# Input stage of a hybrid attention and gating layer put in an order of its own; low weight parts moved from GpSimd to VectorE

## The chip, the cores and the metric

The kernel runs on one core of one Trainium2 chip. The time is the device time of one execution, in microseconds (us). TensorE is called PE in the rows, VectorE DVE, ScalarE ACT, GpSimd POOL, and the queue that issues every transfer SP.

## The reference

One layer over 2048 tokens of width 1024, in float32. One input projection feeds two branches, latent attention and a gated chunk-wise mixing; they are joined, projected and normed.

```python
proj = jnp.einsum('bsd,de->bse', h, w_in)
c_q, c_kv, k_rope, z_a, u, v, z_b = ...
q = rmsnorm(c_q) @ w_uq;  kv = rmsnorm(c_kv) @ w_ukv
q_rope, k_rope = rope(...), rope(...)
attn = causal_attention(concat(q_nope, q_rope), concat(k_nope, k_rope), val)
out_a = attn * silu(z_a)
v = layernorm(gelu(v))
sv = einsum('hts,bcshd->bcthd', tril(w_spatial), v in chunks of 128) + b_spatial
out_b = gelu(u) * sv * silu(z_b)
y = concat(out_a, out_b) @ w_out
return layernorm(alpha * x + y)
```

## The kernel before, in words

Nearly every operand of a product is split into a high part (a rounded copy, made by ScalarE) and a low part (the rest, made by a subtraction, `sub`, line 97), and each product is three matmuls: high by high, high by low, low by high. So each 512-column block of weights or activations that arrives costs one DMA, one ScalarE cast and one subtraction by VectorE or GpSimd.

**Input stage** (a block `ph1`; the first 560 us). It runs in two halves of 1024 tokens (`hf`), each with four parts. (1) The gating vector v: per chunk of 128 tokens 24 matmuls over 512 columns (`tok_mm`, line 791), a Gelu, mean and variance, `rsqrt` with three Newton steps of one-column instructions (`newton`, lines 110 to 112), two multiply-adds (814, 815), a split (821 and 97), 12 matmuls with the spatial weights (833) and four additions of the bias out of PSUM (836). (2) The feature tiles c = 0 to 7 (z_b, u), 24 matmuls over 512 columns each (`feat_mm`, line 798), an activation (942) and a gating product on GpSimd (950, 952). (3) The latents: per 128 tokens 24 matmuls over 416 columns (791 again), a copy (844), norm and rotation on VectorE (846 to 862), four transposes (868, 869) with splits of the result, and from these the queries of all heads (894, 913, 928), which are written to DRAM. (4) Eight more feature tiles (c = 8 to 11, z_a). At the end of the second half stands head 0's preparation: its keys (`k_unit`), the row maxima of its scores (`max_ops`, 352 with VectorE's 359 and 362) and twelve blocks of values (`v_unit`, 310).

These parts are written one after the other in program order (`v_step`, `c_step` with lags SLAG, VLAG, CLAG, and a list `fill` of which some entries are taken after each feature tile); the framework's scheduler then arranges the instructions on each engine. The subtractions for the weights run on GpSimd (`load_w`, `load_wide`), apart from four; those for x run mostly on VectorE. Weights and x pass through five buffers `raw`, so the next transfer waits for the subtraction that empties a buffer.

**Attention and the rest** (`ph2`) do not follow that scheduler: each step is an `Op` with an engine, a cost, a rank and what it depends on, and `issue` plays the program through: at each step it takes the operation that can start first, the lowest rank among near ties, and writes it. Its clock uses a table of costs (`LENGTH`, `LAG`), not the chip.

The lines quoted in the prediction by number are those of this kernel.

Of the kernel before, what the change touches and what calls it, by code (L numbers as in the profile page):

```python
# [56 lines left out]
def hybrid_layer_kernel(ctx: ExitStack, tc: tile.TileContext, xT, x, pos, w_feat, w_v, w_c,  # L57
# [14 lines left out]

    SLAG, VLAG, CLAG = 3, 5, 2
    SKEW, SPLIT, DEFER = 4, 4, 8

    UNITS, YSTART, VLATE = 36, 6, 12
    PREP = (3, 8)
    sb = ctx.enter_context(tc.tile_pool(name="sb", bufs=1))
# [29 lines left out]
    def newton(y, v, t):  # L108

        dve.tensor_scalar(out=t, in0=y, scalar1=y, scalar2=v, op0=ALU.mult, op1=ALU.mult)  # L110
        dve.tensor_scalar(out=t, in0=t, scalar1=-0.5, scalar2=1.5, op0=ALU.mult, op1=ALU.add)
        dve.tensor_scalar(out=y, in0=t, scalar1=y, scalar2=None, op0=ALU.mult)

    def rsqrt(y, v, t):
# [5 lines left out]
        for _ in range(3):  # L120
            for c in range(v.shape[-1]):
                newton(y[:, c:c + 1], v[:, c:c + 1], t[:, c:c + 1])
# [11 lines left out]
    def area16(shape, dt, name):  # L134
        return sb.tile(shape, dt, name=name, tag="area16")
# [30 lines left out]
    def load_kv_w():  # L166
        wkv = att["wkv"] = area12([P, 2, 2, 512], "wkv")
        for i, src in enumerate((w_uk, w_uv)):
            raw = raw2k([P, 512])
            sp.dma_start(out=raw, in_=src)  # L170
            act.copy(out=wkv[:, i, 0], in_=raw)
            sub(dve, wkv[:, i, 1], raw, f(wkv[:, i, 0]))

# [6 lines left out]
    def qs_(h):  # L180
        return q1 if h % 2 else att["q0"][0:DQK + 1]

    def q_alloc():
        att["q0"] = area16([P, 2, S], F32R, "q0")
# [5 lines left out]
    def kslot(h):  # L190
        return kt[h % 3]

    def k_init(i):
        for c in range(2):
            sp.dma_start(out=f(kt[i][NOPE:DQK, c, :]), in_=kr_d[c])
        pool.memset(f(kt[i][DQK:DQK + 1, 0, :]), 1.0)
# [4 lines left out]
    class Op:  # L201


        def __init__(self, eng, cost, rank, fn, deps, lag):
            self.eng, self.cost, self.rank, self.fn, self.lag = eng, cost, rank, fn, lag
            self.deps = [d for d in deps if d is not None]
            self.takes, self.end = [], None


    LENGTH = {"pe": (0.016, 1 / 2400), "act": (0.09, 0.00083), "dve": (0.065, 0.00104), "pool": (0.04, 0.00235),  # L210
              "sp": (0.35, 0.0)}
    LAG = {"pe": 0.2, "act": 0.13, "dve": 0.12, "pool": 0.12, "sp": 3.0}

    COUNT = {"a": 4, "c": 2, "pl": 5, "acc": 2, "acch": 1, "accl": 1, "bsb": 2, "opair": 4, "rb": 1, "raw": 5}

    def issue(ops):

        free = dict.fromkeys(LENGTH, 0.0)
        users, waits = {}, {}
# [5 lines left out]
        taken = {b: [] for b in COUNT}  # L225

        def put(o):
            ready[o.eng].append((max([d.end for d in o.deps], default=0.0), o))
# [4 lines left out]
        for _ in range(len(ops)):  # L233
            best = None
            for e, line in ready.items():
                can = []
                for at, o in line:
# [4 lines left out]
                    if at < float("inf"):  # L242
                        can.append((max(at, free[e]), o))
# [9 lines left out]
            free[o.eng] = t + o.cost  # L253
            o.end = t + o.cost + o.lag
# [6 lines left out]
    work = []  # L261

    def op(eng, n, rank, fn, deps=(), times=1):
        fixed, per = LENGTH[eng]
        o = Op(eng, times * (fixed + per * n), rank, fn, deps, LAG[eng])
        work.append(o)
        return o

    def now():

        for o in work:
            o.fn()
        work.clear()

    def k_ops(pr_, st, rank, deps=()):
# [4 lines left out]
        def mm():  # L280
            st_["x"] = bank_c()
            for i, (w, c) in enumerate(((0, 0), (1, 0), (0, 1))):
                pe.matmul(st_["x"], att["wkv"][:, 0, w, cs], ckv[:, c, ss], start=(i == 0), stop=(i == 2))
# [14 lines left out]
    def k_unit(pr_, st):  # L298
        k_ops(pr_, st, 0)
        now()  # L300

    def v_ops(g, b, rank, deps=()):
# [1063 lines left out]
```

## Time and profile before

| what | value |
|---|---|
| three runs | 1216.54, 1221.67, 1222.01 us, median 1221.67 |
| the profiled execution | 1217.24 us, of it span 1215.5 us |
| TensorE busy, mean granted clock | 1160.4 us, 0.978 |
| VectorE, GpSimd, ScalarE busy | 849.7, 609.4, 584.8 us |

A busy TensorE is not one at its best speed: at half the granted clock the same matmuls count as longer. What a stage can give is read from its idle time and its clock, and from what VectorE does meanwhile.

### The profile page before, as it was taken

To read this page: it belongs to the slowest core of one execution; us is meant where nothing else is said; L and a number is where in the kernel's file an instruction comes from. 1 tells how busy PE (TensorE), PEld (TensorE's weight loads), DVE (VectorE), ACT (ScalarE), POOL (GpSimd) and SP (SyncE) were. 2 spreads that over 40 slices of the span, in tenths; PEclk is the share of its full clock that TensorE was granted. 3 is DMA by queue.
4 is the path that set the end of the run, shared out by engine and by line. 5 is a ranking of instruction groups with operands and counts; after the bars stand their busy time and mean duration, and the time that the engine had idled before them with its cause. 6 is when DMAs were issued, how large, how long until landed. Compare 5 with 4: busy or idle time off the path is not lost.

```text
span 1215.5 us, 17544 instructions
## 1 busy us (share of the span) xinstructions
PE 1160.4 (95%) x5497; PEld 951.8 (78%) x5497; DVE 849.7 (70%) x2314; ACT 584.8 (48%) x1133; POOL 609.4 (50%) x564
## 2 busy tenths in 40 slices
PE   8899999999899999999999999999999879999997
PEld 6678898787688898867877887778777558878886
DVE  4965458525940196476989989889999993458966
ACT  4331412444211323425888878877888774422000
POOL 2353521245332602212979998888899866420000
PEclk9999999999999999997999999999999899999999
DMA  7320322554110503730021212211232224367541
GB/s 243 92 84 15 116 80 74 193 183 130 54 44 18 170 12 125 219 105 27 15 65 49 84 27 63 64 50 37 62 93 66 78 87 138 90 181 240 173 142 61
DMA packets 74765, 116.90 MB, mean 96 GB/s; under 512 B 17248, under 2 KB 21104, under 8 KB 74480
## 3 DMA queue, kind: packets, MB, share of 16 engines
q1 hardware_dynamic: 74672, 115.79, 30.7%
q8 instruction: 43, 0.70, 0.3%
q14 instruction: 50, 0.41, 0.1%
HBM read 79.38 MB, written 36.24 MB: 95 GB/s over the span
## 4 chain that ended last, share of the span: by engine, by line
PE 73%; DVE 14%; DMA 5%; ACT 3%; issue 2%; POOL 2%; SPq 1%; DVEq 0%; POOLq 0%; ACTq 0%
PE bank_a L798 19%; PE bank_a L1134 10%; PE bank_c L352 5%; PE bank_a L432 5%; PE bank_b L476 5%; PE bank_b L477 5%; PE bank_a L433 5%; PE bank_a L434 4%; PE bank_a L791 4%; PE bank_c L1134 4%; DMA raw<-in_xT_dram 2%; PE bank_a L913 2%; DVE gv L814 1%; PE bank_b L833 1%; PE bank_c L310 1%
## 5 line engine op out<-in xcount | busy, mean ns | idle before, releaser
L798 PE MATMUL bank_a<-xbuf,ring 128*128 128x512 f32 x1152 | 270.4, 390 | 0.0
L798 PEld LDWEIGHTS bank_a<-xbuf,ring 128*128 128x128 f32 x1152 | 214.3, 188 | 42.6
L463 POOL TENSOR_TENSOR acc<-acc,xbuf 128x512 f32<-128x512 f32 (+2 forms) x168 | 194.2, 1156 | 32.9 <-ACT xbuf L448 24.5
L442 ACT ACTIVATE bank_a<-bank_a 128x512 f32<-128x512 f32 (+1 forms) x288 | 162.9, 576 | 90.4 <-PE bank_a L434 45.9
L791 PE MATMUL bank_a<-ring,xbuf 128*128 128x512 f32 (+1 forms) x768 | 170.1, 381 | 12.1 <-ACT ring L686 5.7
L97 POOL TENSOR_TENSOR ring<-raw,ring 128x512 fp32r<-128x512 f32 (+1 forms) x76 | 100.4, 1339 | 148.5 <-ACT ring L680 108.7
L791 PEld LDWEIGHTS bank_a<-ring,xbuf 128*128 128x128 f32 x768 | 147.6, 194 | 30.5 <-ACT ring L686 5.7
L97 DVE TENSOR_TENSOR pl<-bank_a,xbuf 128x512 fp32r<-128x512 f32 (+1 forms) x192 | 125.6, 660 | 20.2 <-ACT xbuf L448 18.9
L362 DVE TENSOR_REDUCE mxt<-bank_c 128x1 f32<-128x512 f32 (+1 forms) x192 | 126.8, 666 | 11.6 <-PE bank_c L352 10.0
L477 PE MATMUL bank_b<-pl,xbuf 128*128 128x512 f32 (+1 forms) x320 | 119.6, 377 | 3.5 <-DVE pl L97 3.5
L448 ACT CAST xbuf<-bank_a 128x512 fp32r<-128x512 f32 (+1 forms) x192 | 107.1, 575 | 7.6 <-PE bank_b L476 0.4
L463 POOL TENSOR_TENSOR acc<-acc,ph 128x512 f32<-128x512 f32 (+1 forms) x72 | 85.0, 1181 | 11.7 <-ACT ph L448 8.0
L476 PE MATMUL bank_b<-xbuf 128*128 128x512 f32 (+2 forms) x216 | 82.1, 383 | 3.5 <-ACT xbuf L448 3.5
L942 ACT ACTIVATE act_t<-bank_a 128x512 f32<-128x512 f32 x48 | 28.5, 597 | 117.2 <-PE bank_a L798 117.0
L359 DVE CUSTOM_DVE_ANT_0 bank_c<-bank_c,maskq 128x256 f32<-128x256 f32 (+3 forms) x128 | 65.7, 518 | 13.1 <-PE bank_c L352 12.0
L477 PEld LDWEIGHTS bank_b<-pl,xbuf 128*128 128x128 f32 x320 | 62.2, 194 | 14.2 <-DVE pl L97 5.5
L97 DVE TENSOR_TENSOR pl<-bank_a,ph 128x512 fp32r<-128x512 f32 x96 | 65.1, 683 | 11.6 <-ACT ph L448 10.8
L97 DVE TENSOR_TENSOR xbuf<-raw,xbuf 128x512 fp32r<-128x512 f32 x42 | 33.8, 824 | 48.4 <-ACT xbuf L693 39.9
L432 PE MATMUL bank_a<-xbuf,ring 97*128 97x512 f32 (+2 forms) x160 | 62.0, 388 | 3.2 <-DVE pl L97 3.2
L352 PE MATMUL bank_c<-ring,q 96*128 96x512 f32 (+2 forms) x160 | 61.1, 405 | 3.1 <-DVE xbuf L97 1.6
L432 PE MATMUL bank_a<-q,ring 97*128 97x512 f32 (+2 forms) x160 | 63.0, 394 | 0.0
L352 PE MATMUL bank_c<-ring,xbuf 96*128 96x512 f32 (+2 forms) x160 | 60.1, 391 | 2.3 <-DVE mxt L362 0.9
(209 smaller groups left out, 2388.6 us busy)
## 6 DMA issues: line engine op xcount, KB each, us to landing
raw<-in_w_feat_dram SPq DMA_DIRECT2D x48, 256.0 KB
raw<-in_xT_dram SPq DMA_DIRECT2D x32, 256.0 KB
out_dram<-pl SPq DMA_DIRECT2D x32, 256.0 KB
raw<-in_w_v_dram SPq DMA_DIRECT2D x16, 256.0 KB
ob_d<-act_t SPq DMA_DIRECT2D x16, 256.0 KB
qn_d<-qh SPq DMA_DIRECT2D x16, 256.0 KB
qn_d<-ql SPq DMA_DIRECT2D x16, 256.0 KB
za_d<-act_t SPq DMA_DIRECT2D x16, 256.0 KB
```

What stands on the lines that cost most here:

```text
L97: eng.tensor_tensor(out=out_, in0=a, in1=b, op=ALU.subtract)
L352: pe.matmul(st_["x"][:, :hi - lo], qs_(h)[0:DQK, 0, qb * P:end], kslot(h)[0:DQK, 0, lo:hi], start=True, stop=True)
L362: dve.tensor_reduce(out=mx[h][:, qb, c:c + 1], in_=xps, axis=AX.X, op=ALU.max)
L432: pe.matmul(o_, k_[0:DQK + 1, 0, js], q_[0:DQK + 1, 0, qs], start=True, stop=False)
L442: act.activation(out=o_, in_=o_, func=AF.Exp, scale=SCALE)
L448: act.copy(out=un["ph"][:, c0:512], in_=un["x"][:, c0:512])
L463: pool.tensor_tensor(out=t_["acc"][:, cs], in0=t_["acc"][:, cs], in1=f(p_), op=ALU.add)
L476: pe.matmul(a_ps[:, cs], va, un["ph"][:, ps], start=first, stop=last)
L477: pe.matmul(b_ps[:, cs], vb, un["pl"][:, ps], start=first, stop=last and qt > 0)
L791: pe.matmul(dst[:, :n], a[:, k, js], b[:, 0:4, k, 0:cols], start=(k == 0 and i == 0), stop=(k == KT - 1 and i == 2))
L798: pe.matmul(dst, a[:, slot, k, :], b[:, k, :], start=(k == 0 and i == 0), stop=(k == KT - 1 and i == 2))
L1134: pe.matmul(y, mo(st, k, a)[:, js], wo(k, w)[:, ns], start=(k == kord(st)[0] and i == 0), stop=(k == kord(st)[-1] and i == 2))
```

## The change

All of the input stage is now made of `Op`s too (`manual_schedule`), with ranks from a running time T and costs from the same kind of table, and is played through once at its end (`issue(lead, SLACK)`): transfers may be taken up to 24 us before their rank and the others 16 us, and TensorE work counts as ready 1.2 us after another engine's result. The order of the parts: two feature tiles (c = 0 and 1 of the first 512 tokens) stand ahead of the gating vector; in the first half two z_a tiles stand among the latents; head 0's keys, queries, maxima and nine (not twelve) value blocks get ranks among the last eight z_a tiles, with small weight tiles of their own (`first_weights`); the other seven value blocks come early in attention. The low parts of all feature, v and latent weights and of all of x are made by VectorE; the spatial weights stay on GpSimd, and the full key and value weights go there. `newton` takes both columns of a statistic side by side. Two 16 KB areas become four of 8 KB, the ring of temporaries goes from 12 to 10 buffers with two more `held`, and a load of a head's queries becomes four DMAs where it was two. Attention keeps its rules, but with the new table (a DMA lag of 2.4 where it was 3.0) and with the clock of the input stage running on.

```diff
+    UNITS, YSTART, VLATE = 36, 6, 9
+    MIXLAG, SLACK = 8, 1.2
+    ZA = (3, 6), ()
+    PACE = 0.9
...
+    LENGTH = {"pe": (0.016, 1 / 2350), "act": (0.09, 0.00083), "dve": (0.065, 0.00104), "pool": (0.04, 0.00235),
+              "sp": (0.1, 0.0043)}
+    LAG = {"pe": 0.2, "act": 0.13, "dve": 0.12, "pool": 0.12, "sp": 2.4}
...
+    lead = {"sp": 24.0, "act": 16.0, "dve": 16.0, "pool": 16.0, "pe": 16.0}
...
+            at = [d.end + (slack if o.eng == "pe" != d.eng else 0.0) for d in o.deps]
+            ready[o.eng].append((max(at + [o.rank - lead[o.eng] if lead else 0.0]), o))
...
+            h_ = op("act", n, rank, lambda: act.copy(out=hi(), in_=st_["raw"]), [*last, *before, *deps])
+            l_ = op(eng, n, rank, lambda: sub(engines[eng], lo(), st_["raw"], f(hi())), [h_],
+                    times=1.1 if eng == "dve" else 1.05, pair=True)
+            d_.takes.append((home, [l_]))
...
-                sub(pool, wr_l[:, slot, ks, :], raw, f(wr_h[:, slot, ks, :]))
+                split_in(rank + 2 * q, [P, 4, P], w_feat[c][:, ks, :], lambda ks=ks: wr_h[:, slot, ks, :],
+                         lambda ks=ks: wr_l[:, slot, ks, :], "dve", [("w", slot, k) for k in range(4 * q, 4 * q + 4)])
...
+            g_ = op("act", 512, rank, gelu, [o])
+            s_ = op("dve", 512, rank, stats, [g_], times=4.2)
+            n_ = op("dve", 512, rank, norm, [s_, *of([("sg",)])], times=2.3, pair=True)
+            h_ = op("act", 512, rank, high, [n_], takes=[("tmp", mixed)] * 2)
+            l_ = op("dve", 512, rank, low, [h_], times=1.1, pair=True)
...
+                m_ = op("pe", 256, rank + MIXLAG, lambda half=half: mix(half), [h_, l_, *of([("wsp", half)])], times=7)
+                adds = [op("dve", 256, rank + MIXLAG, lambda half=half, e=e: add(half, e),
+                           [m_, *of([("bsp",), ("area8", t // 4)])]) for e in range(2)]
+                m_.takes.append(("b", adds))
...
+            k_ = op("act", 416, rank, keep, [o])
+            n_ = op("dve", 416, rank, norm, [k_, *of([("gc",), ("rope",)])], times=6.8)
+            t_ = op("pe", 128, rank, turn, [n_], times=6)
+            l_ = op("dve", 512, rank, lows, [h_], times=1.3)
...
+            order = ["f00", "f10", "v0", "v1", "v2", "v3", "v4", "v5", "v6", "v7", "f01", "f11"]
+            if hf == 1:
+                order = ["v0", "v1", "f00", "v2", "f10", "v3", "v4", "v5", "v6", "v7", "f01", "f11"]
...
+                k_ops(0, st, r, deps, "wk0")
...
+                        tops.append(max_ops(0, qb, c, r, [done["q"][0, st], *inits, *k_deps]))
+                        r += PACE * (hi - lo) / 512
...
+        first_head(T0)
+        issue(lead, SLACK)
```

The order on the engines at three places. First **VectorE at the end of the gating vector, first half**, before (`gate` is the mixed chunk with its bias, `vl` the low part of a normed chunk):

```order
L836 TENSOR_TENSOR gate<-bank_b,bsp_bc 64x2x128
L815 SCALAR_TENSOR_TENSOR gv<-gv,sm,sb_bc 128x512
L836 TENSOR_TENSOR gate<-bank_b,bsp_bc 64x2x128
L97 TENSOR_TENSOR vl<-gv,vh 128x512
L836 TENSOR_TENSOR gate<-bank_b,bsp_bc 64x2x128 x2
L97 TENSOR_TENSOR vl<-gv,vh 128x512
L836 TENSOR_TENSOR gate<-bank_b,bsp_bc 64x2x128 x4
L97 TENSOR_TENSOR vl<-gv,vh 128x512
L836 TENSOR_TENSOR gate<-bank_b,bsp_bc 64x2x128 x11
```

and after (`gv` the chunk, `ring<-raw` the low part of a feature weight):

```order
L98 TENSOR_TENSOR vl<-gv,vh 128x512
L897 SCALAR_TENSOR_TENSOR gv<-gv,mv,sg_bc 128x512
L898 SCALAR_TENSOR_TENSOR gv<-gv,sm,sb_bc 128x512
L98 TENSOR_TENSOR ring<-raw,ring 128x512 x2
L98 TENSOR_TENSOR vl<-gv,vh 128x512
L931 TENSOR_TENSOR gate<-bank_b,bsp_bc 64x2x128 x4
L888 BN_STATS st_778<-gv 128x6
L890 BN_AGGR mv<-st_778 128x2
L892 TENSOR_SCALAR sm<-mv 128x1
```

Before, this stretch holds only work of the chunks; now two subtractions for weights stand between two chunks, and the chunk's own work comes as a block.

Second, **TensorE in the latents of the second half**, before (`cn` is the normed chunk of latents, `cq` the query latents):

```order
L791 MATMUL bank_a<-ring,xbuf 128x416 x24
L868 MATMUL bank_c<-ident,cn 128x128 x3
L869 MATMUL bank_c<-ident,cn 32x128
L894 MATMUL bank_a<-uq,cq 128x256 x12
L913 MATMUL bank_a<-cq,uq 128x512 x2
L894 MATMUL bank_a<-uq,cq 128x256 x6
L868 MATMUL bank_c<-ident,cn 128x128 x3
L869 MATMUL bank_c<-ident,cn 32x128
L913 MATMUL bank_a<-cq,uq 128x512 x4
L791 MATMUL bank_a<-ring,xbuf 128x416 x24
```

and after:

```order
L849 MATMUL bank_a<-ring,xbuf 128x416 x21
L1008 MATMUL bank_c<-ident,cn 128x128 x3
L1009 MATMUL bank_c<-ident,cn 32x128
L1082 MATMUL bank_a<-uq,cq 128x256 x6
L849 MATMUL bank_a<-ring,xbuf 128x416 x21
L1008 MATMUL bank_c<-ident,cn 128x128 x3
L1009 MATMUL bank_c<-ident,cn 32x128
L1082 MATMUL bank_a<-uq,cq 128x256 x6
L849 MATMUL bank_a<-ring,xbuf 128x416 x24
L1132 MATMUL bank_a<-cq,uq 128x512 x18
L1008 MATMUL bank_c<-ident,cn 128x128 x3
L1009 MATMUL bank_c<-ident,cn 32x128
```

Before, each chunk's transposes follow one chunk's matmuls, and the queries of four chunks come in one lump; now pieces of the query work stand between the chunks. In this half no feature tile does, before or after.

Third, **TensorE at the end of the input stage** (`bank_c<-ring,q` is a product for the row maxima, `bank_c<-wkv,ckv` a value block), before:

```order
L310 MATMUL bank_c<-wkv,ckv 128x256 x3
L352 MATMUL bank_c<-ring,q_4815 128x512
L352 MATMUL bank_c<-ring,q_4815 128x384
L352 MATMUL bank_c<-ring,q_4815 128x512
L310 MATMUL bank_c<-wkv,ckv 128x256 x3
L352 MATMUL bank_c<-ring,q_4815 128x512 x3
L310 MATMUL bank_c<-wkv,ckv 128x256 x3
L379 MATMUL bank_c<-ident,mrow 4x128
L310 MATMUL bank_c<-wkv,ckv 128x256 x21
```

and after:

```order
L855 MATMUL bank_a<-xbuf,ring 128x512 x6
L345 MATMUL bank_c<-ring,q_4480 128x512 x2
L855 MATMUL bank_a<-xbuf,ring 128x512 x3
L345 MATMUL bank_c<-ring,q_4480 128x512
L855 MATMUL bank_a<-xbuf,ring 128x512 x3
L345 MATMUL bank_c<-ring,q_4480 128x384
L855 MATMUL bank_a<-xbuf,ring 128x512 x3
L345 MATMUL bank_c<-ring,q_4480 128x512 x2
```

Before, these products stand behind the last feature tile, with only each other and the first scores between them; now three matmuls of a z_a tile stand between every one or two of them.

## Rows read from the trace of the kernel before

**Rows 1.** The page, part 1: busy time, share of the span and instructions.

```profile
PE 1160.4 (95%) x5497; PEld 951.8 (78%) x5497; DVE 849.7 (70%) x2314; ACT 584.8 (48%) x1133; POOL 609.4 (50%) x564
```

**Rows 2.** Stretches: length, busy PE, PEld, DVE, ACT, POOL, PEclk, DMA share, GB/s.

```profile
5.69:72.70 67.01, 59.41 (x265) 48.07 (x265) 52.40 (x162) 30.87 (x52) 29.17 (x26) 1.00 0.53 163
185.00:240.00 55.00, 50.94 (x268) 44.73 (x267) 37.94 (x205) 17.83 (x41) 12.66 (x20) 0.97 0.36 128
240.00:332.40 92.40, 85.36 (x389) 71.05 (x388) 49.79 (x145) 35.76 (x61) 40.01 (x37) 0.98 0.40 129
420.50:480.00 59.50, 56.38 (x305) 52.44 (x304) 49.03 (x313) 15.75 (x37) 10.24 (x12) 1.00 0.20 70
537.00:565.00 28.00, 23.66 (x78) 16.46 (x77) 16.27 (x40) 10.40 (x23) 0.00 (x0) 0.64 0.29 77
565.00:1216.00 651.00, 627.27 (x2976) 501.85 (x2974) 536.03 (x1108) 404.43 (x792) 421.23 (x358) 0.98 0.29 88
```

**Rows 3.** Waits of PE in the first 610 us: total, times, longest.

```profile
PE bank_b L833 <- DVE gate L836: 8.3, 5, 5.6
PE bank_a L791 <- DVE csm L112: 4.3, 2, 2.1
```

**Rows 4.** PE in order of time: start, length, instructions.

```profile
79.60 5.61 PE L798 MATMUL bank_a<-xbuf,ring 128*128 128x512 f32 x24
85.05 0.40 PE L833 MATMUL bank_b<-wsp,vh 128*128 128x256 f32 x2
86.46 5.61 PE L798 MATMUL bank_a<-xbuf,ring 128*128 128x512 f32 x24
100.18 8.33 PE L798 MATMUL bank_a<-xbuf,ring 128*128 128x512 f32 x36
434.73 4.88 PE L791 MATMUL bank_a<-ring,xbuf 128*128 128x416 f32 x24
439.45 0.49 PE L868 MATMUL bank_c<-ident,cn 128*128 128x128 f32 x3
...
554.75 1.65 PE L310 MATMUL bank_c<-wkv,ckv 128*128 128x256 f32 x6 [0.28 <-DVE xbuf L97]
556.69 1.65 PE L310 MATMUL bank_c<-wkv,ckv 128*128 128x256 f32 x6 [0.28 <-DVE xbuf L97]
```

**Rows 5.** VectorE in order of time: same columns.

```profile
302.91 0.67 DVE L97 TENSOR_TENSOR vl<-gv,vh 128x512 fp32r<-128x512 f32 x1
313.13 0.69 DVE L808 BATCH_NORM_STATS2 st<-gv 128x6 f32<-128x512 f32 x1
319.94 0.69 DVE L808 BATCH_NORM_STATS2 st<-gv 128x6 f32<-128x512 f32 x1
...
440.81 0.42 DVE L846 BATCH_NORM_STATS2 cst<-cn 128x6 f32<-128x256 f32 x1
446.08 0.41 DVE L846 BATCH_NORM_STATS2 cst<-cn 128x6 f32<-128x256 f32 x1
```

**Rows 6.** Groups by line and shape, first 560 us: busy us, mean ns | idle before.

```profile
L97 POOL TENSOR_TENSOR ring<-raw,ring 128x512 fp32r<-128x512 f32 x60 | 82.5, 1390 | 147.8 <-ACT ring L680 108.7 <-ACT ring L686 25.2 <-PE bank_a L798 8.0
L97 POOL TENSOR_TENSOR ring<-raw,ring 128x416 fp32r<-128x416 f32 x16 | 17.9, 1146 | 0.8 <-ACT ring L686 0.8
L97 DVE TENSOR_TENSOR vl<-gv,vh 128x512 fp32r<-128x512 f32 x16 | 13.8, 864 | 0.1
```

**Rows 7.** Waits of the DMA queue in the first 565 us: total, times, longest.

```profile
SPq L679 <- POOL ring L97: 82.7, 30, 34.7
```

**Rows 8.** Short stretches: same columns as in group 2.

```profile
0.00:20.00 20.00, 14.31 (x49) 11.29 (x50) 8.19 (x12) 11.03 (x18) 7.15 (x21) 1.00 0.71 233
300.00:320.00 20.00, 13.10 (x63) 11.02 (x61) 18.47 (x64) 2.20 (x4) 0.00 (x0) 0.91 0.00 1
540.00:550.00 10.00, 7.61 (x19) 4.08 (x19) 7.78 (x17) 1.66 (x5) 0.00 (x0) 0.73 0.51 123
550.00:560.00 10.00, 8.49 (x30) 6.51 (x29) 4.56 (x12) 3.20 (x10) 0.00 (x0) 0.50 0.01 3
```


## What the change should do to the time

> **What bounds the kernel now.** I read the page's busy times first, then the busy time and clock by stretch, then what TensorE waits for, then TensorE and VectorE in order of time. TensorE is busy 1160 of 1215.5 us [rows 1], so only its idle time and its slow clock can be won, and the change touches those up to about 565 us. Behind that, attention and the output lose 24 us of idle time in 651 us [rows 2], which the change leaves nearly alone. The profiled execution took 1217.24 us; the median of the three runs shown, 1221.67, is 4.4 us longer.
>
> At full clock a feature tile of 24 matmuls takes 5.45 us (79.60 to 85.05), so 0.227 us for 512 columns, the 12 mixing matmuls of a chunk take 1.41 us, 0.117 us for 256 columns, and the 24 matmuls of a chunk of latents 4.7 us [rows 4]. The losses of the input stage, from group 2 where not said:
>
> - Gating vector, first half (5.69 to 72.70): 67.01 - 59.41 = 7.6 us idle.
> - Latents, first half (185 to 240): 55.0 - 50.9 = 4.1 us, and 3% of the clock, 1.6 us. Together 5.7.
> - Gating vector, second half (240 to 332.4): 92.4 - 85.4 = 7.0 us, and 2% of the clock, 1.9 us. Together 8.9.
> - Latents, second half (420.5 to 480): 3.1 us.
> - End of the stage (537 to 565): 4.3 us idle at a mean clock of 0.64. The 78 matmuls there are 36 of the value blocks (4.2 us), a dozen row maxima (2.4 us) and 30 others of some 0.19 us, 5.8: 12.4 us at full clock. So 15.6 us are lost of 28.
>
> The sum is 40.9 us. Who ends these waits is VectorE: the additions behind the mixing, 8.3 us, and the Newton steps of the latents, 4.3 us [rows 3].
>
> **What decides the first four.** In the gating vector VectorE is full: one chunk follows the other at 313.13 and 319.94, every 6.81 us [rows 5], while TensorE needs 5.45 + 1.41 = 6.86 us for it. In the latents a chunk costs VectorE 5.27 us (440.81 to 446.08) [rows 5] and TensorE 4.7 + 0.66. So the two engines are level, and whatever more VectorE is given is time unless TensorE has other work in that stretch. The new plan counts less for VectorE than the rows show: by its table an operation of 512 elements costs 0.065 + 0.00104 x 512 = 0.597, so a gating chunk costs (4.2 + 2.3 + 1.1) x 0.597 + 4 x 0.331 = 5.87 us, 0.94 too little, and a chunk of latents 6.8 x 0.498 + 1.3 x 0.597 = 4.16, 1.1 too little. Over eight chunks the real VectorE falls 8 to 9 us behind the plan, and TensorE, which must follow the written order, waits there.
>
> **The parts.**
>
> *Low parts to VectorE.* GpSimd loses 60 subtractions of 1390 ns, 16 of 1146 [rows 6], and eight for x, some 110 us; VectorE gains 84. One in VectorE, alone, takes 0.67 us (302.91) [rows 5], so some 55 us. GpSimd's time was on no path but that of the buffers: the queue of transfers waited 82.7 us for these subtractions [rows 7], and TensorE's waits on loads were short. So the first costs nothing and gains little; the second lies beside feature tiles, where VectorE is mostly idle, except for those in the gating stretches: 8 for x and 2 to 5 for weights.
>
> The vl subtraction takes 0.67 us alone and 864 ns in the mean of the half where GpSimd is busy too [rows 5, 6]; so an empty GpSimd speeds VectorE a little, and I take the undisturbed 0.67. The Trainium skill (Trace Analysis, Optimizing Scalar/DVE Operations) says that the two share a port into SBUF, so that moving work between them might not help: it speaks against this part. By it the 84 subtractions would keep 0.86 us, some 20 of them in the full stretches, and the sum below would be 10 and not 14.
>
> *Gating, first half.* Two feature tiles now come first, while the v weights arrive. 20 transfers of 256 KB at 233 GB/s [rows 8] take 22.5 us; with the start, a cast and the last matmuls VectorE gets its first chunk at about 28. Then 8 x 6.81 and ten subtractions of 0.67 make 61.2; some 1.6 of it (the last additions) lie behind the last mixing, and some 4 us are added by handing over: the last mixing ends at about 92. By then TensorE has done eight chunks and 93 feature matmuls, 285 x 0.227 + 8 x 1.41 = 76 us, so 16 are lost. Before, the last mixing ends at 100.18 [rows 4] with 120 feature matmuls done, 82 us, so 18 are lost. Gain 2.
>
> *Latents, first half.* Two z_a tiles among them, 11 us of other work, cover VectorE's lag of 9. Idle under 1 us for 5.7: gain 4.7.
>
> *Gating, second half.* VectorE starts some 9 us into the part (24 + 15 matmuls); 8 x 6.81 and 13 subtractions make 63.2, less 1.6, plus 4: the last mixing comes after 75 to 77 us, with 66 us of TensorE work written ahead of it. Some 10 lost for 8.9: gain -1.
>
> *Latents, second half.* No features among them. Newton's steps now stand alone where the scheduler had mixed two chunks: between 5.27 and 6.2 us per chunk, I take 5.9, since each dependent step shows. Some 3.5 us lost for 3.1: gain 0.
>
> *End.* The maxima now have 24 matmuls between few of them, so VectorE keeps up (40 maxima, each about the 0.69 us of its other pass over 512 elements [rows 5], 27 us under 43.6 us of TensorE's eight tiles). Nine value blocks at the end still go through two PSUM buffers at 0.97 us each (554.75 to 556.69 is two) [rows 4], some 8 us for 6 us of TensorE work in them; the way of the last queries through DRAM costs some 2, and a short spell at half clock 3. Some 7 lost for 15.6: gain 8.6. Three value blocks move into attention, 9 x 0.117 = 1 us of TensorE work that is done in either place.
>
> *Attention's table and the added DMAs.* A shorter lag for DMAs may put a wait where none was: between -3 and +3 us, by the 24 us of idle time that are there; I take 0.
>
> The sum is 2 + 4.7 - 1 + 0 + 8.6 = 14 us: 1203 on the profiled execution's footing, 1208 on the median's. I forecast **1205**, between the two. Unknowns of 4 us for handing over, of 0.9 us per chunk in the latents and of 3 in attention bound this case to 1194 to 1214.
>
> **The rivals.**
>
> *The waits go almost wholly.* If VectorE's real pace is nearer the plan, since GpSimd no longer disturbs it and loads are always ahead, what is left is 8 of the 40.9 us. Gain 33: 1184 to 1189. For it: 28 us of loss at VectorE's pace are all in stretches with feature tiles close by. Against it: 6.81 us is already a stretch in which GpSimd stood still (0.00 busy) [rows 8].
>
> *It gives back what it gains.* The end wins 8, and VectorE's subtractions and bare Newton steps lose 5 to 8 in the gating and latent parts. Gain 3 or less: 1214 to 1221. The rows speak for it as far as VectorE is full there; against it speaks that the waits before had the same cause and feature tiles now lie among the first half's latents.
>
> *Slower: the clock.* TensorE fell to half its clock (0.50, that is 1.2 GHz) between 550 and 560 after a stretch in which it was busy 7.6 of 10 us, and stayed there although it was busy 8.5 of 10 [rows 8]. In the new order the gating parts, some 64 and 68 us, are filled with waits of 1 to 2 us at every chunk. If the clock goes there, each lost tenth of its mean costs 13 us; below 0.89 the gain of 14 is gone, and at 0.78 the kernel is 15 us slower, 1232. Against it: 300 to 320, busy 13.1 of 20, kept 0.91 [rows 8]. The Trainium skill (TensorE: Matmul & The Clock Gate, HAM oscillation) tells of kernels in which small idle gaps between groups of matmuls made the clock go down and up again and again; by that this case is the likelier one, and the row of 300 to 320 does not bear it out.
>
> **How the numbers follow.** Forecast 0.47, waits gone 0.22, given back 0.18, slower 0.13. A measurement of this kernel tells about 0.5%, 6 us, from no change: faster means under 1215.6, slower over 1227.8. Faster gets the forecast but 0.02, all of the second case and 0.04 of the third: 0.71. Same gets 0.02 + 0.14 + 0.01: 0.17. Slower: 0.12. The range leaves out the better half of the second case and most of the last: 1186 to 1222; the forecast's own is 1194 to 1214.
>
> **What would show it.** Right: attention's dense part starts near 550 and not 565; TensorE waits for VectorE's additions and Newton steps in both gating parts, with some 7 and 10 us idle; no stretch of half clock longer than some 8 us near the end; VectorE's chunk still near 6.8 us. Wrong: a gating part without idle time (the second case); a granted clock under 0.9 in a gating part (the last); or a change of more than 5 us behind the start of attention.

## The result: slower, and the profile after

The changed kernel takes **1236.0 us** in the median of four runs (1231.08 to 1238.81); the kernel before, on the same chip, 1220.0. The ratio is 1.013, its 95% interval 1.0086 to 1.0173. The forecast was 1205 in a range of 1186 to 1222, with a chance of 0.12 for slower: wrong in sign and outside the range. The slowdown is under 2%, but its interval lies clear of no change. The profiled execution is one of 1231.08 us, 5 under the median.

The page's part 1 of the changed kernel:

```profile
PE 1159.9 (94%) x5497; PEld 942.7 (77%) x5497; DVE 916.5 (75%) x2398; ACT 589.8 (48%) x1137; POOL 504.4 (41%) x482
```

Against [rows 1] GpSimd lost 105 us and VectorE gained 67 (forecast 110 and 55); TensorE is as busy as before, within 0.5 us. So the 13.9 us by which the span grew (1215.5 to 1229.4) are idle time of TensorE. The stretches of the changed kernel that answer to [rows 2] (length, then busy PE, PEld, DVE, ACT, POOL, clock, DMA):

```profile
5.73:96.00 90.27, 83.17 (x382) 67.01 (x383) 74.04 (x197) 34.65 (x57) 7.11 (x12) 0.98 0.33 108
180.00:245.00 65.00, 58.72 (x305) 50.39 (x304) 51.35 (x284) 16.39 (x41) 6.11 (x14) 1.00 0.25 83
260.00:360.00 100.00, 89.08 (x411) 72.02 (x410) 71.22 (x190) 36.76 (x60) 7.05 (x12) 0.98 0.32 103
435.70:506.00 70.30, 60.02 (x318) 53.18 (x317) 62.66 (x334) 16.39 (x44) 10.41 (x18) 0.99 0.24 80
500.00:520.00 20.00, 17.22 (x73) 13.92 (x74) 12.20 (x32) 8.68 (x16) 0.86 (x2) 0.91 0.47 134
540.00:572.00 32.00, 29.87 (x147) 23.75 (x146) 13.96 (x31) 9.31 (x21) 4.76 (x18) 1.00 0.41 129
572.00:1230.00 658.00, 630.51 (x2997) 502.11 (x2995) 539.69 (x1117) 411.58 (x800) 423.60 (x358) 0.98 0.30 88
```

Idle are 7.1, 6.3, 10.9 and 10.3 us in the gating vector and latents of the two halves; the end of the stage, once at a mean clock of 0.64, now runs at full clock with 2.1 us idle. The clock is at 0.98 or more in all these stretches but one: from 500 to 520, where head 0's preparation begins, it is 0.91. What TensorE waits for in the first 600 us (total, times, longest):

```profile
PE bank_c L1008 <- DVE cn L995: 8.7, 7, 1.9
PE bank_b L927 <- DVE vl L98: 7.7, 9, 2.4
PE bank_b L927 <- DVE gate L931: 7.6, 5, 1.7
PE bank_a L855 <- ACT xbuf L705: 7.0, 2, 5.7
PE bank_c L283 <- DVE ring L98: 3.9, 1, 3.9
```

The transpositions wait for the normed latents (`cn`), the mixing for a chunk's low part (`vl`) and for its own additions, head 0's first keys for a low part: all VectorE. The row of ScalarE (`ACT`) is the first wait of the kernel, 5.7 of its 7.0 us. The two largest of VectorE in [rows 3] were 8.3 and 4.3 us.

**A ledger by work done.** The stretches hold different work in the two orders. Both kernels issue the same 5497 matmuls, so I added these up in order of time, each at its length at full clock (0.227 us for 512 columns [rows 4], others by their columns, the masks of 128 bfloat16 columns 0.04), and read how far the wall clock is behind the sum (1078.6 us at the last matmul). What each stretch of work loses in us (idle time, half clock, and short matmuls that take longer than their columns):

| work done, us | what is in it | before | after | gained | forecast |
|---|---|---|---|---|---|
| 0 to 150 | start, gating 1, features | 19.5 | 21.2 | -1.7 | +2 |
| 150 to 250 | latents 1 | 10.4 | 15.0 | -4.6 | +4.7 |
| 250 to 375 | gating 2, features | 9.4 | 15.4 | -6.0 | -1 |
| 375 to 475 | latents 2 | 9.1 | 20.7 | -11.6 | 0 |
| 475 to 525 | end, head 0 | 19.8 | 6.7 | +13.1 | +8.6 |
| from 525 | attention, output | 60.8 | 63.9 | -3.1 | 0 |

The end brought more than forecast. The four stages in which VectorE sets the pace lost 23.9 us, where 5.7 of gain stood in the sum. The stages are cut by work done, so the row of latents 2 reaches to 547 us in the changed kernel: the 3.9 us for which head 0's first keys wait and the spell at half clock beside it (500 to 520) are in it too. No run undoes the order at the end, the two early feature tiles or the smaller ring of buffers by itself; what they bring is read from this table alone.

**VectorE's rows say why.** One gating chunk of the changed kernel in order of time (start, length):

```profile
321.75 0.68 DVE L888 BATCH_NORM_STATS2 st<-gv 128x6 f32<-128x512 f32 x1
...
323.25 0.27 DVE L113 TENSOR_SCALAR sm<-sm 128x1 f32<-128x1 f32 x1
323.56 0.15 DVE L115 TENSOR_SCALAR sm<-sm 128x1 f32<-128x1 f32 x1
323.75 0.21 DVE L117 TENSOR_SCALAR sm<-sm 128x1 f32<-128x1 f32 x1
324.00 0.27 DVE L113 TENSOR_SCALAR sm<-sm 128x1 f32<-128x1 f32 x1
...
325.37 0.68 DVE L98 TENSOR_TENSOR vl<-gv,vh 128x512 fp32r<-128x512 f32 x1
```

The statistics of one chunk, 14 instructions of which twelve have one column, fill 321.75 to 325.37, 3.62 us, and nothing else stands among them: a Newton step takes 0.75 us (323.25 to 324.00), and each of its instructions begins only when the one before has ended. With two multiply-adds (1.5), the low part (0.69) and four additions (1.75) a chunk is 7.6 us, and with the subtractions between them the chunks come every 8.1 us in the mean (first half, starts at 29.8 to 86.8, seven steps) and 8.3 us (296.9 to 354.7). Before, the same instructions took 6.81 [rows 5], with additions of another chunk among the dependent steps, though not among the last ones:

```profile
315.61 0.43 DVE L836 TENSOR_TENSOR gate<-bank_b,bsp_bc 64x256 f32<-64x256 f32 x1
316.07 0.15 DVE L118 TENSOR_SCALAR sm<-sm 128x1 int32<-128x1 int32 x1
316.25 0.42 DVE L836 TENSOR_TENSOR gate<-bank_b,bsp_bc 64x256 f32<-64x256 f32 x1
316.60 0.26 DVE L110 TENSOR_SCALAR sm<-sm 128x1 f32<-128x1 f32 x1
```

A chunk of latents of the changed kernel:

```profile
446.52 0.61 DVE L987 BATCH_NORM_STATS2 cst<-cn 128x6 f32<-128x256 f32 x2
...
448.18 0.46 DVE L113 TENSOR_SCALAR csm<-csm 128x1 f32<-128x1 f32 x2
448.56 0.27 DVE L115 TENSOR_SCALAR csm<-csm 128x1 f32<-128x1 f32 x2
448.74 0.33 DVE L117 TENSOR_SCALAR csm<-csm 128x1 f32<-128x1 f32 x2
448.99 0.45 DVE L113 TENSOR_SCALAR csm<-csm 128x1 f32<-128x1 f32 x2
...
451.98 0.42 DVE L98 TENSOR_TENSOR cq<-bank_c,cq 128x256 fp32r<-128x256 f32 x1
452.32 0.28 DVE L98 TENSOR_TENSOR ckv<-bank_c,ckv 128x128 fp32r<-128x128 f32 x1
452.52 0.27 DVE L98 TENSOR_TENSOR krs<-bank_c,krs 32x128 fp32r<-32x128 f32 x1
452.72 0.60 DVE L987 BATCH_NORM_STATS2 cst<-cn 128x6 f32<-128x256 f32 x2
```

6.2 us from chunk to chunk (446.52 to 452.72), 6.8 for the next, with the rotation of a block of queries in it. In the kernel before, at 5.27 [rows 5], the scheduler had put the rotation, the low parts of the chunk ahead and even the next chunk's first instructions between the dependent steps.

### The profile page after: what moved, and what is told of

It is laid out like the page before. It is cut to its first block, busy times and chain, and to the rows that moved or that the text cites. A ratio compares the mean times of both kernels' runs of the same rounds, so it can differ in the third digit from the quotient of the medians.

```text
span 1229.4 us, 17596 instructions
## 1 busy us (share of the span) xinstructions
PE 1159.9 (94%) x5497; PEld 942.7 (77%) x5497; DVE 916.5 (75%) x2398; ACT 589.8 (48%) x1137; POOL 504.4 (41%) x482
## 4 chain that ended last, share of the span: by engine, by line
PE 67%; DVE 20%; DMA 4%; issue 3%; ACT 3%; POOL 1%; SPq 0%; DVEq 0%; ACTq 0%; POOLq 0%
PE bank_a L855 19%; PE bank_a L1327 10%; PE bank_c L345 5%; PE bank_a L849 5%; PE bank_a L418 4%; PE bank_b L463 4%; PE bank_b L462 4%; PE bank_a L419 4%; PE bank_a L420 4%; PE bank_c L1327 3%; DVE gate L931 2%; DVE csm L113 1%; DVE pl L98 1%; DVE sm L113 1%; DVE ring L98 1%
## 5 line engine op out<-in xcount | busy, mean ns | idle before, releaser
L855 PE MATMUL bank_a<-xbuf,ring 128*128 128x512 f32 x1152 | 280.5, 396 | 7.0 <-ACT xbuf L705 7.0
L855 PEld LDWEIGHTS bank_a<-xbuf,ring 128*128 128x128 f32 x1152 | 216.7, 190 | 52.6 <-ACT xbuf L705 8.1
L449 POOL TENSOR_TENSOR acc<-acc,xbuf 128x512 f32<-128x512 f32 (+2 forms) x168 | 194.8, 1160 | 21.2 <-ACT xbuf L434 12.7
L849 PE MATMUL bank_a<-ring,xbuf 128*128 128x512 f32 (+1 forms) x768 | 173.9, 377 | 1.7 <-DVE ql L98 1.7
L849 PEld LDWEIGHTS bank_a<-ring,xbuf 128*128 128x128 f32 x768 | 144.3, 191 | 19.6 <-DVE ql L98 2.2
L98 DVE TENSOR_TENSOR ring<-raw,ring 128x512 fp32r<-128x512 f32 (+1 forms) x88 | 71.1, 820 | 99.7 <-ACT ring L705 91.5
L355 DVE TENSOR_REDUCE mxt<-bank_c 128x1 f32<-128x512 f32 (+1 forms) x192 | 126.7, 666 | 21.4 <-PE bank_c L345 19.6
L98 DVE TENSOR_TENSOR pl<-bank_a,xbuf 128x512 fp32r<-128x512 f32 (+1 forms) x192 | 125.6, 660 | 17.9 <-ACT xbuf L434 16.5
L98 DVE TENSOR_TENSOR pl<-bank_a,ph 128x512 fp32r<-128x512 f32 x96 | 65.0, 684 | 16.5 <-ACT ph L434 15.6
L98 POOL TENSOR_TENSOR held<-qrt 128x128 f32<-128x128 f32 x16 | 7.4, 461 | 151.3 <-DVE qrt L1092 149.0
L957 POOL TENSOR_TENSOR gate<-gate,held 128x512 f32<-128x512 f32 x8 | 11.0, 1392 | 132.0 <-DVE gate L931 103.0
L705 ACT CAST ring<-raw 128x512 fp32r<-128x512 f32 (+1 forms) x72 | 41.9, 601 | 46.0 <-PE bank_a L855 23.0
```

The costliest lines, as they stand in the source:

```text
L98: eng.tensor_tensor(out=out_, in0=a, in1=b, op=ALU.subtract)
L355: dve.tensor_reduce(out=mx[h][:, qb, c:c + 1], in_=xps, axis=AX.X, op=ALU.max)
L449: pool.tensor_tensor(out=t_["acc"][:, cs], in0=t_["acc"][:, cs], in1=f(p_), op=ALU.add)
L849: pe.matmul(dst[:, :n], a[:, k, js], b[:, 0:4, k, 0:cols], start=(k == 0 and i == 0), stop=(k == KT - 1 and i == 2))
L855: pe.matmul(dst, a[:, slot, k, :], b[:, k, :], start=(k == 0 and i == 0), stop=(k == KT - 1 and i == 2))
```

## The experiments

Three theories were set against each other. **Bare chains**: an operation of the plan is a whole block, so VectorE's dependent steps stand bare and its chunk is longer. **Costs of the plan**: VectorE is counted too cheap, so the written order asks for its results too early. **Moved subtractions**: VectorE has 84 more of them. The measured times are medians with the ratio to the kernel before, run on the same chip, and its 95% interval. The runs come from two chips and several sessions, in which the kernel before took 1217.3 to 1220.0 us; differences between two runs are of their medians, and a few us of them can be due to that. The losses are those of the ledger, each read from one profiled execution.

**One part undone, and that part alone.** `low_parts_back` returns the low parts of the weights (those of x stay) to GpSimd in the changed kernel, `low_parts_alone` moves them, and those of x, in the kernel before:

```diff
-                         lambda ks=ks: wr_l[:, slot, ks, :], "dve", ...
+                         lambda ks=ks: wr_l[:, slot, ks, :], "pool", ...
```

> The changed kernel with the low parts of the feature, latent and v weights made by GpSimd again (the first four v weights stay on VectorE, as in the kernel before). Theory 'bare chains' (VectorE's dependent statistics stand one behind the other: 7.6 us for a gating chunk where the kernel before took 6.81, some 6.3 for a chunk of latents where it took 5.27): within 5 us of the changed kernel, 1230 to 1238 us, because only some ten of these subtractions of 0.7 us stand in the stretches where VectorE is full. Theory 'moved subtractions' (84 of 0.7 to 0.8 us on VectorE are what TensorE waits for): back to the kernel before or below it, 1212 to 1222. Theory 'costs of the plan' (VectorE counted too cheap, so that TensorE's order asks too early): no change, 1232 to 1238.

Measured 1252.7 us, 1.0292 (1.0266 to 1.0318): outside every range, and worse than the changed kernel. By the ledger it loses more in every stage of the input up to 525 us of work, most at the start (28.5 for 21.2). Why it is so much slower is taken up again below.

```diff
-                sub(pool, wr_l[:, slot, ks, :], raw, f(wr_h[:, slot, ks, :]))
+                sub(dve, wr_l[:, slot, ks, :], raw, f(wr_h[:, slot, ks, :]))
```

> The kernel before with that one part of the change: all low parts of feature, latent and v weights and of x on VectorE. 'Moved subtractions': slower by 8 to 15 us, 1228 to 1235. 'Bare chains' and 'costs of the plan': within 5 us of the kernel before, 1215 to 1225, because the scheduler still fills the chains.

Measured 1217.2 us, 1.0002 (0.9986 to 1.0019). So the move costs nothing in the old order, and in the new one it is a help; the third theory falls. The group of a chunk's low part in the changed kernel, then in `low_parts_back`:

```profile
L98 DVE TENSOR_TENSOR vl<-gv,vh 128x512 fp32r<-128x512 f32 x16 | 11.0, 686 | 0.9 <-ACT vh L902 0.7
```

```profile
L98 DVE TENSOR_TENSOR vl<-gv,vh 128x512 fp32r<-128x512 f32 x16 | 12.5, 781 | 3.0 <-ACT vh L902 2.9
```

864 ns before [rows 6], 686 with GpSimd emptied, 781 with it filled again. These means mix two kinds: before, eleven of the sixteen take 0.66 to 0.75 us, and five, each begun while GpSimd was at work, 1.06 to 1.37 (a pair of rows stands in the last section); in `low_parts_back` two of sixteen are slow, 1.15 and 1.69. The forecast's 0.67 was the right value for a subtraction that GpSimd does not hold up. The Trainium skill (Perfetto Trace Analysis, Optimizing Scalar/DVE Operations) says that moving work between the two might not help because they share a port. The slow rows beside a busy GpSimd agree with the shared port, and the ratio of 1.0002 agrees with "might not help"; in the new order the move is worth the 17 us between `low_parts_back` and the changed kernel.

**The plan's counts.** `true_costs` leaves the instructions and corrects what they are counted at:

```diff
-            s_ = op("dve", 512, rank, stats, [g_], times=4.2)
+            s_ = op("dve", 512, rank, stats, [g_], times=6.2)
...
-            n_ = op("dve", 416, rank, norm, [k_, *of([("gc",), ("rope",)])], times=6.8)
+            n_ = op("dve", 416, rank, norm, [k_, *of([("gc",), ("rope",)])], times=10.8)
```

> The changed kernel with VectorE's costs as the trace of it shows them (statistics of a gating chunk 3.7 us where 2.5 was counted, norm and rotation of a latent chunk 5.4 where 3.4 was, its low parts 0.98 where 0.78 was, an addition of the bias 0.44 where 0.33 was). Same instructions, another order. 'Costs of the plan': most of the waits go, 1205 to 1220. 'Bare chains': VectorE's work is the same, TensorE gets at most 5 us, 1228 to 1238. 'Moved subtractions': the same, 1230 to 1238.

Measured 1224.9 us, 1.0063 (1.0042 to 1.0083): 11 us less than the changed kernel, between the two ranges. By the ledger it wins 8 and 9 us in the two latent stages and next to nothing in the gating stages (0.2 and 1.9), but loses 20.4 at the end for 6.7, where TensorE now waits 4.5 us for maxima and falls to half its clock for a time (two stretches of its profile, columns as above):

```profile
520.00:540.00 20.00, 16.14 (x64) 12.35 (x63) 9.64 (x23) 4.42 (x7) 1.11 (x6) 0.83 0.26 90
...
560.00:575.00 15.00, 13.96 (x63) 10.89 (x62) 9.68 (x26) 10.03 (x21) 3.50 (x3) 0.75 0.22 67
```

A part of the cause, not the whole: in the latents most of what was lost comes back when the count alone is right, in the gating vector hardly any. Why the end suffers is not shown.

With it and the next runs goes a small change of buffers (the rotated queries take theirs with the transposition, so that the plan does not block itself). `early_buffers` has that alone:

```diff
-            h_ = op("act", 512, rank, high, [mm], takes=[("tmp", freed)])
+            h_ = op("act", 512, rank, high, [mm], takes=[] if early else [("tmp", freed)])
...
+                mm.takes += [("tmp", freed)] * 2
```

> A control: the changed kernel with only the one thing that true_costs and chains_opened share beside their own edit, the rotated queries' two buffers taken with their transposition and not one by one behind it. Both theories: within 5 us of the changed kernel, 1231 to 1241. If it is below 1230, that much of the gain of the other two is its.

1235.6 us, 1.0135 (1.0086 to 1.0184): no effect of its own can be seen.

**VectorE's length, with the order held.** `two_steps` shortens the chains and moves nothing (a probe: it leaves out one step of each reciprocal square root):

```diff
-        for _ in range(3):
+        for _ in range(2):
             newton(y, v, t)
```

> The changed kernel with two Newton steps instead of three in the input stage (one step of each reciprocal square root is left out); the order is the same, instruction for instruction, but for the 16 x 3 + 16 x 6 that are missing. VectorE's bare chain is then 0.75 us shorter per gating chunk and 0.80 per latent chunk, 25 us in all. 'Bare chains' (VectorE's own length is what TensorE waits for in this order): TensorE gets more than half of it, 1216 to 1223. 'Order alone' (TensorE's instructions are written in the wrong places, and VectorE's length is of no account): under 5 us, 1231 or more.

Measured 1210.9 us, 0.9931 (0.9909 to 0.9952), below both ranges. 16 x 0.75 + 16 x 0.80 = 25 us less of VectorE, 25 us less in the kernel: in this order the pace is VectorE's, almost one for one. The plan still counted what it counted before, so the order is as early as it was; "order alone" falls. The run does not part "bare chains" from "costs of the plan": a shorter VectorE also comes nearer to what the plan counts for it.

**The chains opened.** `chains_opened` makes every VectorE instruction of statistics, norm, rotation and latent low parts an operation of its own:

```diff
-            s_ = op("dve", 512, rank, stats, [g_], times=4.2)
-            n_ = op("dve", 512, rank, norm, [s_, *of([("sg",)])], times=2.3, pair=True)
+            s_ = op("dve", 512, rank, moments, [g_])
+            j_ = op("dve", 2, rank, join, [s_], times=2)
+            o = guess_ops(yq, vq, tq, 1, op("dve", 1, rank, above, [j_]), rank)
+            o = newton_ops(yq, vq, tq, slice(0, 1), o, rank)
+            c_ = op("dve", 512, rank, centred, [j_, *of([("sg",)])], times=1.2, pair=True)
+            n_ = op("dve", 512, rank, scaled, [c_, o, *of([("sg",)])], times=1.2, pair=True)
```

> The changed kernel with every VectorE instruction of the statistics, norms, rotations and latent low parts as an operation of its own in the plan, with its length and lag, so that other work can stand between two dependent ones. 'Bare chains': VectorE's gating chunk falls from 7.6 to 7.0 us or less and its latent chunk from 6.3 to 5.3, 16 x 0.6 + 16 x 1.0 = 26 us of VectorE, of which TensorE gets 12 to 22: 1212 to 1224. 'Costs of the plan': what true_costs gives and no more. 'Moved subtractions': 1230 or more.

Measured **1192.7 us**, 0.9814 (0.9779 to 0.9849): 43 us under the changed kernel (39 by the two ratios), twice the expected gain. VectorE in order of time, where two chunks now run through each other:

```profile
300.97 0.45 DVE L882 TENSOR_SCALAR sm<-sm 128x1 f32<-128x1 f32 x2
301.35 0.27 DVE L884 TENSOR_SCALAR sm<-sm 128x1 f32<-128x1 f32 x2
301.53 0.33 DVE L886 TENSOR_SCALAR sm<-sm 128x1 f32<-128x1 f32 x2
301.78 0.45 DVE L882 TENSOR_SCALAR sm<-sm 128x1 f32<-128x1 f32 x2
...
309.75 0.27 DVE L882 TENSOR_SCALAR sm<-sm 128x1 f32<-128x1 f32 x1
309.94 0.68 DVE L914 BATCH_NORM_STATS2 st<-gv 128x6 f32<-128x512 f32 x1
310.54 0.14 DVE L884 TENSOR_SCALAR sm<-sm 128x1 f32<-128x1 f32 x1
310.71 0.42 DVE L966 TENSOR_TENSOR gate<-bank_b,bsp_bc 64x256 f32<-64x256 f32 x1
```

Two chunks' Newton steps take 0.81 us together (300.97 to 301.78) where one took 0.75. The gating chunks come every 6.6 and 6.2 us. What is left of the largest waits of TensorE in the first 600 us, and two stretches, gating 2 and latents 2:

```profile
PE bank_a L856 <- ACT xbuf L705: 7.1, 3, 5.6
PE bank_b L962 <- DVE gate L966: 1.3, 3, 0.9
PE bank_c L1074 <- DVE cn L1037: 1.0, 1, 1.0
```

```profile
260.00:345.00 85.00, 84.65 (x415) 70.83 (x416) 70.18 (x202) 37.84 (x63) 10.06 (x14) 1.00 0.37 117
405.00:475.00 70.00, 68.33 (x363) 61.38 (x363) 62.88 (x342) 22.14 (x55) 11.10 (x18) 1.00 0.25 84
```

Idle 0.4 and 1.7 us. `latents_opened` has the same edit for the latents alone:

```diff
-            n_ = op("dve", 416, rank, norm, [k_, *of([("gc",), ("rope",)])], times=6.8)
-            t_ = op("pe", 128, rank, turn, [n_], times=6)
+            t_ = op("pe", 128, rank, turn, norm_ops(k_, rank), times=6)
```

> chains_opened with the gating chunks' statistics closed again, so only the latent chunks are opened (and counted at their true length). 'Bare chains': the latents lose what they lost before or less, the gating parts stay as in the changed kernel; of the 43 us between the changed kernel and chains_opened about 25 come, 1207 to 1216. If the gain needs both (a plan whose clock is right from beginning to end): under 12 us, 1224 or more.

Measured 1218.2 us, 0.9997 (0.9973 to 1.0020), 17 us less than `early_buffers`: between the two ranges, 2 us outside the first. The ledger by stage, of this run and of others that the text comes to:

| run | 0-150 | 150-250 | 250-375 | 375-475 | 475-525 | from 525 |
|---|---|---|---|---|---|---|
| after | 21.2 | 15.0 | 15.4 | 20.7 | 6.7 | 63.9 |
| two_steps | 15.9 | 9.4 | 9.3 | 15.6 | 7.8 | 63.5 |
| true_costs | 21.0 | 7.3 | 13.5 | 11.7 | 20.4 | 60.9 |
| latents_opened | 21.4 | 6.9 | 16.2 | 8.4 | 8.5 | 65.4 |
| chains_opened | 12.7 | 7.0 | 1.2 | 9.2 | 7.5 | 65.4 |
| opened_cheap | 18.2 | 8.9 | 6.9 | 13.8 | 10.1 | 65.9 |
| low_parts_back | 28.5 | 18.9 | 16.5 | 26.1 | 9.7 | 64.4 |
| opened_old_table | 11.7 | 7.5 | 1.0 | 9.1 | 10.0 | 59.2 |
| opened_both_za | 11.2 | 7.3 | 1.8 | 5.3 | 16.9 | 58.5 |

With the latents opened the latent stages lose what they lost before the change or less (6.9 and 8.4), and the gating stages stay where the change had put them (21.4 and 16.2); those go only with their own chains. From here to `chains_opened` the times differ by some 25 us, and the gating stages by 24. That is more than twice what VectorE itself was expected to save there (16 x 0.6 us), so the moment at which TensorE asks seems to have its part in it; the next run looks at that.

**Open, or rightly counted?** `opened_cheap` keeps the chains open and counts their steps at 0.6:

```diff
+                o = plain(*a, **k)
+                o.cost, o.lag = 0.6 * o.cost, 0.6 * o.lag
```

> chains_opened with the small instructions of the opened chains (aggregates left out) counted in the plan at 0.6 of their length and lag, so that a chunk's statistics are again counted about as short as in the changed kernel. Same instructions, still one operation each. 'What counts is that the chain is open': within 6 us of chains_opened, 1187 to 1199. 'What counts is that the plan has the right length': half of the gain or more goes, 1210 or more.

Measured 1207.7 us, 0.9909 (0.9885 to 0.9934), between the two ranges: of the 43 us, 28 come though the length is wrong, 15 (12 by the ratios) need the right length. Both theories hold a part. With `true_costs` (right length, closed: 11) they roughly add up.

**The low parts once more**, in `chains_opened`, with the edit of `low_parts_back`:

> chains_opened with the low parts of the feature, latent and v weights (but for four) on GpSimd, as in low_parts_back, which lost 17 us against the changed kernel. If GpSimd's subtractions slow the order by themselves (later weights, VectorE's two-operand instructions slowed beside them, 686 to 781 ns for the low part of a chunk): 1200 to 1210. If they did so only because VectorE's closed chains were the pace: within 5 us of chains_opened, 1188 to 1198. If VectorE gains from the 60 us that it sheds: 1187 or less.

Measured 1207.3 us, 0.9913 (0.9885 to 0.9941), 15 us slower than `chains_opened` (12 by the ratios) and in the first range. VectorE is not slowed in the chunks here (the low part takes 686 ns, the chunks come every 6.3 us). TensorE's waits of the first 600 us name, as they did not in `chains_opened`:

```profile
PE bank_a L850 <- POOL ring L98: 1.6, 2, 0.9
PE bank_a L856 <- POOL ring L98: 1.6, 1, 1.6
```

Weights come later, with GpSimd's subtraction between a transfer and its matmul. These are 3.2 of some 15 us. That the plan arranges everything else anew around GpSimd is a likely rest, but no run takes it apart: why the low parts cost 15 to 17 us on GpSimd in the new order stays open in the main.

**Attention's table.** `opened_old_table` and `changed_old_table` give attention its old table and a clock from nought, in `chains_opened` and in the changed kernel:

```diff
+        free.update(dict.fromkeys(free, 0.0))
...
+        LENGTH.update(pe=(0.016, 1 / 2400), sp=(0.35, 0.0))
+        LAG["sp"] = 3.0
```

> chains_opened with attention planned by the table of the kernel before (a transfer's lag 3.0, its cost 0.35) and with a clock of its own that begins at nought. Behind 500 us of TensorE work chains_opened loses 67.9 us against 62.3 in the kernel before. 'The table and the running clock cost 5 us': 1186 to 1189. 'What attention loses more has another cause' (other first blocks, chance in how waits fall): 1190 to 1196.

> The changed kernel with attention planned by the old table and a clock from nought, nothing else. 'The table and the running clock cost attention 4 to 6 us in the change too': 1229 to 1232. 'Only in chains_opened': 1234 to 1238.

Measured **1187.1 us**, 0.9738 (0.9697 to 0.9779), and 1231.0 us, 1.0101 (1.0078 to 1.0123). Behind 525 us of work the profiled executions lose 59.2 and 60.5 us, where `chains_opened` and the changed kernel lose 65.4 and 63.9. So 3 to 6 us of attention's loss seem to be the new table and the running clock, in both. The first pair's intervals touch, the second's overlap, and a single execution of each tells: the three ledgers with the old table read 58.5 to 60.5, those with the new one 60.9 (`true_costs`) to 65.9. `opened_old_table` is the fastest kernel of this study, 2.6% under the kernel before.

**A miss.** `opened_both_za` adds z_a tiles among the second half's latents:

```diff
-    ZA = (3, 6), ()
+    ZA = (3, 6), (3, 6)
```

> opened_old_table with two z_a tiles among the latents of the second half too, as the changed kernel has them in the first half alone. Between 375 and 475 us of TensorE work opened_old_table still loses 9 us there, in the first half 5 to 8. 'The second half's latents lack other work': 1181 to 1185. 'What is lost there lies at the beginning of head 0's preparation': 1186 or more.

1189.5 us, 0.9767 (0.9743 to 0.9790): no gain, and in the second range. By the ledger the latents lose 5.3 us where `opened_old_table` lost 9.1, as the first theory had it, but the end loses 16.9 for 10.0. The tiles taken to the latents are missing among head 0's maxima (72 feature matmuls stand behind the first maximum, 105 in `opened_old_table`), which is the likely reason: work that fills one hole is taken from another.

## Why the prediction was wrong

- **VectorE's time per chunk ("8 x 6.81", "I take 5.9") and what hides it in the latents: the step that failed.** 6.81 us was read from the trace as what a chunk costs VectorE. It is what a chunk costs in an order that puts other work between dependent instructions. Put together as a block the same instructions take 7.6 us, and the first half's term would have been 8 x 7.6 + 6.7 = 67.5 us and not 61.2. The last mixing ended at 96 where 92 was forecast. I had found that the plan counts 5.87 for 6.81; the real gap was 1.7 us per chunk, and 2.0 us per chunk of latents (6.2 for 4.16).
- **Where it cost most: the latents.** Between the forecast gain of 14 and the measured loss of 14 lie 28 us; 21 of them are the two latent stages, 9 the two gating stages, 3 attention, and the end made good 4.5. In the second half "some 3.5 us lost" stood; with 6.2 to 6.8 us against TensorE's 4.7 + 0.66 the same sum gives 7 to 11, and 10.3 were idle. The right idea (Newton's steps stand bare) had the wrong size, a block of queries that is rotated too was left out, and the idea was used in one place only: the gating chunks have the same chain, and there the old pitch was kept. The plan's short count was seen too, but taken as covered in the first half and as no more than those 3.5 us in the second; with the count alone put right (`true_costs`) the two latent stages lose 19 us where they lost 36.
- **"Two z_a tiles among them ... cover VectorE's lag": wrong.** In an order written out, work covers a wait only if it stands ahead of the waiting instruction. In the first half three of the seven waits of transpositions fall, 3.5 of the 8.7 us, with matmuls of a z_a tile (L855) or of the latents (L849) right behind them:

```profile
192.00 0.73 PE L849 MATMUL bank_a<-ring,xbuf 128*128 128x416 f32 x3
193.75 0.52 PE L1008 MATMUL bank_c<-ident,cn 128*128 128x128 f32 x3 [1.02 <-DVE cn L995]
...
194.51 0.94 PE L855 MATMUL bank_a<-xbuf,ring 128*128 128x512 f32 x3
```

  Forecast was under 1 us idle and a gain of 4.7; 6.3 us were idle, and the ledger has -4.6.
- **VectorE as the pace setter, right**, and more strictly than thought: 25 us off VectorE are 25 us off the kernel. But it should have given slower, not a rival of 3 us of gain. No rival held "slower because VectorE's chunk itself gets longer"; "it gives back what it gains" named the bare Newton steps and priced them, with the subtractions, at 5 to 8 us for 32 chunks, where the four stages lost 24.
- **The subtractions at 0.67, right** (686 ns), and at no cost in the old order (1.0002). The 864 ns were misread, though: they are the mean of both halves and not of one, and most of the sixteen took 0.67 there too.
- **End of the stage, right in kind, too small**: +13.1 for +8.6. The maxima lie among the tiles, and of the 20 us at half clock only a short spell is left (the stretch of 500 to 520, at 0.91).
- **Attention, 0 within -3 to +3**: -3.1, at the edge. With the old table it loses 60.5 us, as before (60.8); that rests on single traces.
- **The clock's rival did not come about.** The mean granted clock rose from 0.978 to 0.985; the waits of up to 2.4 us at the chunks left the gating stretches at 0.98. The Trainium skill (TensorE: Matmul & The Clock Gate, A second HAM failure mode: psum-queue depth-cycling) tells of a kernel in which short idle spells between groups of matmuls made the clock go up and down; the gating stretches here, at 0.98, show little of it.

## What to carry to other kernels

A time per chunk that is read from a scheduled trace belongs to that order, not to the instructions: before a block is written out as one piece, add its dependent steps from start to start. When a plan replaces a scheduler, its smallest operation should be the instruction where chains are long, with length and lag apart; here that was worth 43 us, some 12 to 15 of them for the right length, and turned a loss of 1.3% into a gain of 1.9%, and 2.6% with attention's old table. Shorten the suspected engine without moving anything first (one Newton step less): it tells in one run whether the kernel follows that engine. Whether its work is too long or only counted too short takes a second run, with the count alone put right.

## What the runs showed of the hardware that was not expected

- A one-column instruction of VectorE that needs the result of the one before starts 0.04 us after that one's end (323.25 + 0.27, then 323.56; 323.56 + 0.15, then 323.75), so 0.19 to 0.31 us after its start, and the trace shows no larger gap on VectorE meanwhile. Two such chains through each other take 0.81 us per pair of steps, one alone 0.75: the second is nearly free, so a busy VectorE need not be at its best pace.
- A 512-column subtraction of VectorE with both operands in SBUF took 0.66 to 0.69 us beside an idle GpSimd. The five slow ones of the sixteen in the kernel before began while GpSimd was in the middle of such an instruction, and each ended 0.55 us after that instruction's end, as if it had waited for it: below, 86.38 + 1.37 = 87.75, where GpSimd's ends at 87.21. Yet taking 84 subtractions off GpSimd changed the kernel before by 0.0002.

```profile
85.92 1.29 POOL L950 TENSOR_TENSOR gate<-gate,act_t 128x512 f32<-128x512 f32 x1 [4.54 <-ACT act_t L942]
86.38 1.37 DVE L97 TENSOR_TENSOR vl<-gv,vh 128x512 fp32r<-128x512 f32 x1
```
